# GDN heads of a hybrid GLA / gated DeltaNet block: output with values on the partitions, norm sums on 32x32 blocks

## The chip, the cores and the metric

The kernel runs on one core of one Trainium2 chip. The metric is the device time of one execution in microseconds, as the median of the runs shown. The core has five engines with a queue of instructions each: TensorE (PE; its weight loads are listed as PEld), VectorE (DVE), ScalarE (ACT), GpSimd (POOL) and SyncE (SP). DMAs are issued from the queues of SP, ACT and POOL. All data is float32; large products are made in three passes from a high and a low part of each operand (float32r), small ones directly in float32, which the trace shows as two passes ("x2").

## The reference, cut to what matters

The block takes 1024 tokens of 1024 channels through a GLA branch, a gated DeltaNet (GDN) branch, a gated merge and an MLP. The change concerns the end of the GDN branch: 8 heads with 128 keys and 128 values each. Per head, in chunks (the kernel uses chunks of 128 tokens, eight of them):

```python
v_new = uu - einsum('bhcd,bhdv->bhcv', ww, state)
o = einsum('bhcd,bhdv->bhcv', qd, state) + einsum('bhij,bhjv->bhiv', at, v_new)
state = dc[..., None, None] * state + einsum('bhcd,bhcv->bhdv', ks, v_new)
...
o_d = rms_norm(o_d, gdn_onorm_w) * jax.nn.silu(d_g.reshape(bsz, s, GDN_HEADS, GDN_DV))
y_d = o_d.reshape(bsz, s, GDN_V) @ w_branch_gdn
```

`rms_norm` divides each token of a head by the root of the mean square over its 128 values. The queries are L2-normalised in the reference; the kernel leaves the query unnormalised and brings its sum of squares in at the norm of the output instead: the sum of squares of the output over 128, plus the query's sum of squares (with its own epsilon) times 128 epsilon, is what the root is taken of.

## The kernel before, in words

All products are interleaved by a clock. `dense_b` (L475) makes one 128x1024 projection tile: for each of eight k it issues six matmuls of 512 columns and then calls `tick()` (L382), which adds one to the clock and issues everything that is due. `at(dt, fn)` (L371) puts a function on the agenda for `dt` steps ahead; what is due at the same step is issued in the order in which it was registered. In `gdn_head` (L906) `on(t, fn)` means step `t` counted from the head's own beginning.

One head takes 24 steps, three projections of eight steps: query, value, gate (`psq`, `psv`, `psg`). What the head does with them reaches into the steps of the next head: its state chain runs from step 24 to 47, and its finish behind that. So step 53 of one head is step 29 of the next one's chain. A head's instructions:

- steps 0 to 17: loads of the solved key matrices, of the decay and of two rows spread over all partitions (`eg`, `ke`, L1012 to L1016), the convolution of the query (`conv_silu`, three VectorE operations on 1024 columns), scores `attT` (L979).
- steps 15 to 33: the query's sums of squares. ScalarE squares into `qj`, VectorE transposes 32x32 blocks and sums (`token_part`, L992, steps 28 and 30), a product with `quad`, a matrix of 32x32 identities, adds up the four blocks of 32 partitions (`token_total`, L1000), and four VectorE operations bring that to one column per chunk, `vq`.
- steps 24 to 47, the chain: `c0(t)`, `c1(t)`, `c2(t)` (L1033 to L1070) at steps 24+3t, 25+3t, 26+3t for chunk t. `c0` transposes the values on TensorE and adds `ke` times the state, ScalarE scales that to `rs`; `c1` multiplies by the solved matrix `U`, ScalarE makes `vn` twice (scaled, and plain); `c2` makes the state's product (`kt`), VectorE writes the new state `st` from it (for t = 0 ScalarE copies it), and then the output `po` of the chunk, with `attT` and the decayed query `qd` as weights and `vn` and the old state as the moving operand: tokens on the partitions, values along the row. The state that VectorE writes at step 26+3t is needed by `c0` at step 27+3t.
- steps 35 and 47: `results` (L1075): ScalarE squares each 128x128 block of the output with a sum (`so`), and copies `po` to `ob`.
- step 26 to 28: the gate `sg` (ScalarE's tanh, then two VectorE operations).
- step 48 `norm` (L1083), eleven VectorE operations on 128x8; step 50 `scale`, one of 128x1024; steps 52 and 53 `fin` (L1092), four transposes on TensorE each; VectorE multiplies their result by the norm's weight and the gate into `sg` in two operations (steps 53, 54); step 56 the store to `od_d`.

Head 6 finishes later: `late` moves its second `results` by 7 steps, `end` its norm by 27, `f_` its `fin` by 32; head 7's `fin` is moved by 6. After head 7 the branch products begin (`branch`, L1698; `gla_plan`, L1596): step 24 of head 7 is their step 0, each of the seven products has eight steps of six matmuls, and their operands are split by ScalarE (`x_cast`, `w_cast`) and VectorE (`x_low`, `w_low`).

From the first GDN head on TensorE, VectorE and ScalarE keep the written order (L1454); SP and GpSimd do from head 7 on (L1797), before that a planner at compile time places their DMAs where its own estimate has them ready. Tiles come from shared pools: 30 tiles of 128x1024 in the pool `w4`, 16 of which hold the normalised input until the last projection, two `U`; four PSUM banks in `pa`, four more as two pairs in `pm`.

Of the kernel before, what the change touches and what calls it, by code (L numbers as in the profile page):

```python
# [20 lines left out]
EPS = 1e-6  # L21
# [29 lines left out]
def block_kernel(ctx: ExitStack, tc: tile.TileContext, x, c, ada_w, ada_b, pre_mix_w, post_mix_w,  # L51
# [36 lines left out]
            DMA.dma_start(dbg[name] if dst is None else dst(dbg[name]), src)  # L88


    def rsqrt(v, n):

        if n == 64:
            r, t = t4((128, n), p="rs"), t4((128, n), p="rt")
        else:
            r, t = small(n, "rs"), small(n, "rt")
        V.tensor_scalar(t.bitcast(I32), v.bitcast(I32), 1, None, ALU.logical_shift_right)
        V.tensor_scalar(r.bitcast(I32), t.bitcast(I32), -1.0, float(0x5F3759DF), ALU.mult, ALU.add)

        V.tensor_mul(t, r, r)  # L100
        V.tensor_mul(t, t, v)
        V.scalar_tensor_tensor(t, t, -10.0 / 3, t, ALU.add, ALU.mult)
        V.scalar_tensor_tensor(r, t, 5.0, r, ALU.add, ALU.mult)
        V.tensor_mul(t, r, r)
        V.scalar_tensor_tensor(t, t, -27.0 / 1024, v, ALU.mult, ALU.mult)
        last["rs"] = V.scalar_tensor_tensor(r, t, 9.0 / 16, r, ALU.add, ALU.mult).ins
        return r
# [794 lines left out]

    oa_d = [dr.tile([2, 128, 1024], F32, name=f"oa_d{i}") for i in range(4)]
    od_d = [dr.tile([2, 128, 1024], F32, name=f"od_d{i}") for i in range(4)]

    def gdn_head(h, then=None):  # L906

# [65 lines left out]
        psq = dense_b(h_rhs)  # L973

        q = conv_silu(psq, h, 8)
        vq = small(8, "vq")
        z = {}

        def att(hf):  # L979
# [17 lines left out]
            V.transpose(z["t"][:, h_], z["qj"][:, h_])  # L997
            V.reduce_sum(z["r"][:, hf * 16:(hf + 1) * 16], r3(z["t"][:, h_], 16), axis=mybir.AxisListType.X)

        def token_total():  # L1000
            ps = pat()
            T.matmul(ps[:, 0:32], quad.rearrange("p a b -> p (a b)"), z["r"], start=True, stop=True)

            def columns():
                for i in range(4):
                    V.tensor_scalar(vq[32 * i:32 * i + 32],
                                    ps[32 * i:32 * i + 32, 0:32].rearrange("p (t c) -> p c t", c=4)[:, i], EPS, None, ALU.add)

            on(33, columns)

        ktok, eg = t4(p="kt", tag="hd"), t4(p="eg")
        DMA.dma_start(ktok, kt_d[h])  # L1012
        DMA.dma_start(eg, gc_d[h].partition_broadcast(128))
# [9 lines left out]
        on(15, lambda: V.tensor_tensor(qd, q, eg, ALU.mult))  # L1023
        on(28, lambda: token_part(0))
        on(30, lambda: token_part(1))
        on(32, token_total)
        psv = dense_b(h_rhs)

        vv = conv_silu(psv, 16 + h, 16, 1)
        so = small(8, "so")  # L1030
        c = {"st": None}

        def c0(t):  # L1033
# [18 lines left out]
        def c2(t):  # L1052
            sl = slice(t * 128, (t + 1) * 128)
            i, hf, st, vs, vn = t % 4, t // 4, c["st"], c["vn"][:, 0:128], c["vn"][:, 128:256]
            if t < NT - 1:
                pS = c["pv"][:, 256:384]
                T.matmul(pS, ktok[:, sl], vs, start=True, stop=True)
                sn = c["st"] = sm.tile([128, 128], F32, tag="st", name=nm("st"), bufs=3)
                if t:
                    V.scalar_tensor_tensor(sn, st, decB[:, h * 8 + t:h * 8 + t + 1], pS, ALU.mult, ALU.add)  # L1060
                else:
                    A.copy(sn, pS)
            if i == 0:
                c["po"] = pat()
            po = c["po"]
            T.matmul(po[:, i * 128:(i + 1) * 128], z["att"][:, sl], vn, start=True, stop=(t == 0))
            if t:
                T.matmul(po[:, i * 128:(i + 1) * 128], qd[:, sl], st, start=False, stop=True)
            if i == 3:
                on(47 + late if hf else 35, lambda: results(hf, po))  # L1070

# [3 lines left out]
        def results(hf, po):  # L1075
            if not hf:
                c["ob"] = t4(p="ob")
            for t in range(hf * 4, hf * 4 + 4):
                A.activation(c["ob"][:, t * 128:(t + 1) * 128], po[:, t % 4 * 128:(t % 4 + 1) * 128], AF.Square,
                             accum_out=so[:, t:t + 1])  # L1080
            A.copy(c["ob"][:, hf * 512:(hf + 1) * 512], po)

        def norm():  # L1083

            V.tensor_scalar(so, so, 1.0 / 128, None, ALU.mult)
            V.scalar_tensor_tensor(so, vq, 128.0 * EPS, so, ALU.mult, ALU.add)
            c["rf"] = rsqrt(so, 8)

        def scale():
            V.tensor_tensor(r3(c["ob"]), r3(c["ob"]), colb(c["rf"], 8), ALU.mult)  # L1090

        def fin(hf):  # L1092
            pt, h_ = pat(), slice(hf * 512, (hf + 1) * 512)
            for i in range(4):
                t = hf * 4 + i
                T.transpose(pt[:, i * 128:(i + 1) * 128], c["ob"][:, t * 128:(t + 1) * 128], ident)
            on(53 + f_ + hf, lambda: V.scalar_tensor_tensor(sg[:, h_], pt, don, sg[:, h_], ALU.mult, ALU.mult))
            if hf:
                on(56 + f_, lambda: (DMA if h == 7 else A).dma_start(od_d[h // 2][h % 2], sg))
                dump("odT", sg, lambda t: t[h * 128:(h + 1) * 128, :])  # L1100

        for t in range(NT):
            on(24 + 3 * t, lambda t=t: c0(t))
# [1 line left out]
            on(26 + 3 * t, lambda t=t: c2(t))  # L1105
        if then:
            then()
        on(48 + end, norm)
        on(50 + end, scale)
        on(52 + f_, lambda: fin(0))  # L1110
        on(53 + f_, lambda: fin(1))
        psg = dense_b(h_rhs)

        sg = t4(p="si")
# [1359 lines left out]
```

## Time and profile before

| | us |
|---|---|
| median of 3 runs (lowest, highest) | 1893.22 (1891.84, 1896.31) |
| profiled execution, device time | 1890.98 |
| its span, first to last instruction | 1889.3 |
| TensorE busy | 1864.9 (99%) |
| VectorE busy | 1376.1 (73%) |
| ScalarE busy | 893.7 (47%) |
| GpSimd busy | 149.7 (8%) |

The GDN heads lie between about 570 and 978 us, the branch products behind them. TensorE's granted clock is 0.999 over the span. In rows of the order in time the columns are: start, time from the first start to the last end of the row, engine, source line (always the line of the helper that issues), operation, output and inputs by the program's names, sizes, and how many instructions the row holds; in brackets, how long the engine had been idle and what ended that. `pa` and `pm` are the PSUM tiles. `kt` is the `c2` product for the state, `ident,ob` the transposes of `fin`, `sqr,quad` the product of `token_total`, `si` the tile of the gate, `cv` that of a convolution.

### The profile page before, as it was taken

How to read it: one execution, taken by the hardware profiler on the slowest of the kernel's cores; microseconds unless marked ns; L12 is line 12 of the kernel's file. 1: busy time of each engine (PE TensorE's matmuls, PEld its weight loads, DVE VectorE, ACT ScalarE, POOL GpSimd, SP SyncE). 2: the span in 40 equal slices, each digit the busy share in tenths (PEclk: the TensorE clock that was granted, in tenths of full speed). 3: DMA queues.
4: the chain of work that ended last, by engine and by line, in shares of the span. 5: the costliest groups of instructions: out<-in, count | busy, mean ns of one | idle time of the engine just before them, and what ended most of it. 6: DMA issues, size and time to landing. Idle time of an engine off the chain costs nothing. (4 is left out here: it accounts for less than half of the span.)

```text
span 1889.3 us, 26430 instructions
## 1 busy us (share of the span) xinstructions
PE 1864.9 (99%) x10169; PEld 1563.8 (83%) x10169; DVE 1376.1 (73%) x2127; ACT 893.7 (47%) x1619; POOL 149.7 (8%) x138
## 2 busy tenths in 40 slices
PE   7999999999999999999999999999999999999998
PEld 5788888989898888888888888878888888888886
DVE  5664834868766666766788778976788877777887
ACT  5574324252333444444664555578644446433333
POOL 2120110110110000000101001000021220000001
PEclk9999999999999999999999999999999999999999
DMA  9685673223124444443869666246667668252425
GB/s 310 219 258 184 160 145 102 68 80 122 56 80 150 129 132 137 133 134 123 257 169 240 200 157 197 80 155 225 221 203 237 231 213 318 71 223 105 163 101 100
DMA packets 252318, 311.17 MB, mean 165 GB/s; under 512 B 72514, under 2 KB 178192, under 8 KB 252192
## 3 DMA queue, kind: packets, MB, share of 16 engines
q1 hardware_dynamic: 222464, 274.67, 45.2%
q0 software_dynamic: 13456, 19.80, 6.0%
q10 hardware_dynamic: 16272, 15.02, 2.4%
q8 instruction: 80, 1.31, 0.3%
q14 instruction: 46, 0.38, 0.1%
HBM read 229.05 MB, written 80.39 MB: 164 GB/s over the span
## 5 line engine op out<-in xcount | busy, mean ns | idle before, releaser
L38 PE MATMUL pm<-hH,wH 128*128 128x512 f32 x864 | 286.7, 413 | 0.0
L38 PE MATMUL pm<-hL,wH 128*128 128x512 f32 x864 | 268.6, 392 | 0.0
L38 PE MATMUL pm<-hH,wL 128*128 128x512 f32 x864 | 267.4, 391 | 0.0
L38 PE MATMUL pm<-oH,wB 128*128 128x512 f32 x672 | 214.7, 394 | 0.0
L38 PE MATMUL pa<-w,yH 128*128 128x512 f32 (+1 forms) x696 | 212.3, 387 | 0.0
L38 PEld LDWEIGHTS pm<-hL,wH 128*128 128x128 f32 x864 | 162.2, 188 | 36.5
L38 PEld LDWEIGHTS pm<-hH,wL 128*128 128x128 f32 x864 | 162.1, 188 | 36.4
L38 PEld LDWEIGHTS pm<-hH,wH 128*128 128x128 f32 x864 | 145.1, 190 | 17.0 <-issue 0.2
L38 DVE TENSOR_TENSOR w<-raw,w 128x512 fp32r<-128x512 f32 (+1 forms) x144 | 125.6, 875 | 41.5 <-ACT w L38 40.5
L38 PEld LDWEIGHTS pa<-w,yH 128*128 128x128 f32 x696 | 130.2, 188 | 26.7 <-DVE ya L38 0.4
L38 PEld LDWEIGHTS pm<-oH,wB 128*128 128x128 f32 x672 | 126.2, 188 | 26.0 <-DMA wB<-in_w_branch_gla_dram 0.5
L38 ACT CAST w<-raw 128x512 fp32r<-128x512 f32 (+1 forms) x144 | 99.6, 712 | 89.3 <-DVE raw L38 80.2
L38 PE MATMUL pa<-w,yL 128*128 128x512 f32 (+1 forms) x348 | 134.6, 387 | 0.0
L38 PE MATMUL pm<-oL,wB 128*128 128x512 f32 x336 | 131.0, 390 | 0.0
L38 PE MATMUL pa<-oB,w 128*128 128x512 f32 x480 | 112.1, 391 | 2.4 <-ACT oB L38 1.1
L38 ACT CAST wH<-raw 128x1024 fp32r<-128x1024 f32 x62 | 64.5, 1048 | 97.3 <-PE pm L38 48.7
L38 PEld LDWEIGHTS pa<-oB,w 128*128 128x128 f32 x480 | 89.7, 188 | 22.2 <-DVE oB L38 1.8
L38 DVE SCALAR_TENSOR_TENSOR cv<-pm,ccol,cv 128x1023 f32<-128x1023 f32 (+2 forms) x72 | 92.1, 1279 | 13.7 <-ACT cv L38 12.3
L38 DVE TENSOR_TENSOR wL<-raw,wH 128x1024 fp32r<-128x1024 f32 x62 | 75.4, 1220 | 34.6 <-ACT wH L38 34.5
L38 PE MATMUL pm<-oT,w 128*128 128x512 f32 x384 | 90.8, 389 | 0.0
L38 PE MATMUL pa<-oT,w 128*128 128x512 f32 x384 | 90.8, 389 | 0.0
L38 DVE TENSOR_TENSOR ya<-pa,ya 128x512 f32<-128x512 f32 (+1 forms) x83 | 55.9, 682 | 43.7 <-PE pa L38 43.7
(402 smaller groups left out, 3739.4 us busy)
## 6 DMA issues: line engine op xcount, KB each, us to landing
yL<-y_d SPq DMA_DIRECT2D x53, 512.0 KB, 7.1
raw<-in_mlp_w_dram SPq DMA_DIRECT2D x23, 1024.0 KB, 6.1
raw<-in_w_in_dram SPq DMA_DIRECT2D x18, 1024.0 KB, 7.3
raw<-in_w_in_dram SPq DMA_DIRECT2D x32, 512.0 KB, 4.9
araw<-in_ada_w_dram SPq DMA_DIRECT2D x32, 512.0 KB, 3.9
raw<-in_mlp_w_dram SPq DMA_DIRECT2D x18, 512.0 KB, 5.8
araw<-in_ada_w_dram SPq DMA_DIRECT2D x32, 256.0 KB, 6.4
sl<-sg_d SPq DMA_DIRECT2D x16, 512.0 KB, 7.1
```

Of the source, the lines that this page charges most:

```text
L38: r = fn(*args, **kw)
```

## The change

In `c2` weights and moving operand change places: the output is made with values on the partitions and tokens along the row. The transposes of `fin` and the product with `quad` with its four column reads are gone. `results` copies only, and squares the whole head at once when its second half is there (`sqo`). The squares are transposed and summed in blocks of 32x32 by VectorE, as the query's are (`turn`, `sums`, steps 49 to 52). `norm` (step 53) adds the query's sums, brings the four blocks of partitions together with three copies and three additions on 32x32, takes the root there in the nine operations of `rsqrt`, transposes the block and stores it to a row of 1024 in DRAM (`on_d`, one for each head). `rows` (step 57) loads that row into all 128 partitions; `scale` (step 55) multiplies output, weight and gate into `sg`, and `fin` (step 62) multiplies `sg` by the row; the store follows at step 63. The shifts `late`, `end` and `f_` of heads 6 and 7 stay as they are.

```diff
--- before.py
+++ after.py
@@ -88,9 +88,11 @@
             DMA.dma_start(dbg[name] if dst is None else dst(dbg[name]), src)
 
 
-    def rsqrt(v, n):
-
-        if n == 64:
+    def rsqrt(v, n, rt=None):
+
+        if rt:
+            r, t = rt
+        elif n == 64:
             r, t = t4((128, n), p="rs"), t4((128, n), p="rt")
         else:
             r, t = small(n, "rs"), small(n, "rt")
@@ -902,6 +904,7 @@
 
     oa_d = [dr.tile([2, 128, 1024], F32, name=f"oa_d{i}") for i in range(4)]
     od_d = [dr.tile([2, 128, 1024], F32, name=f"od_d{i}") for i in range(4)]
+    on_d = [dr.tile([1024], F32, name=f"on_d{h}") for h in range(8)]
 
     def gdn_head(h, then=None):
 
@@ -973,7 +976,6 @@
         psq = dense_b(h_rhs)
 
         q = conv_silu(psq, h, 8)
-        vq = small(8, "vq")
         z = {}
 
         def att(hf):
@@ -996,17 +998,6 @@
             h_ = slice(hf * 512, (hf + 1) * 512)
             V.transpose(z["t"][:, h_], z["qj"][:, h_])
             V.reduce_sum(z["r"][:, hf * 16:(hf + 1) * 16], r3(z["t"][:, h_], 16), axis=mybir.AxisListType.X)
-
-        def token_total():
-            ps = pat()
-            T.matmul(ps[:, 0:32], quad.rearrange("p a b -> p (a b)"), z["r"], start=True, stop=True)
-
-            def columns():
-                for i in range(4):
-                    V.tensor_scalar(vq[32 * i:32 * i + 32],
-                                    ps[32 * i:32 * i + 32, 0:32].rearrange("p (t c) -> p c t", c=4)[:, i], EPS, None, ALU.add)
-
-            on(33, columns)
 
         ktok, eg = t4(p="kt", tag="hd"), t4(p="eg")
         DMA.dma_start(ktok, kt_d[h])
@@ -1023,11 +1014,10 @@
         on(15, lambda: V.tensor_tensor(qd, q, eg, ALU.mult))
         on(28, lambda: token_part(0))
         on(30, lambda: token_part(1))
-        on(32, token_total)
         psv = dense_b(h_rhs)
 
         vv = conv_silu(psv, 16 + h, 16, 1)
-        so = small(8, "so")
+        so = small(32, "so", 2)
         c = {"st": None}
 
         def c0(t):
@@ -1063,9 +1053,9 @@
             if i == 0:
                 c["po"] = pat()
             po = c["po"]
-            T.matmul(po[:, i * 128:(i + 1) * 128], z["att"][:, sl], vn, start=True, stop=(t == 0))
+            T.matmul(po[:, i * 128:(i + 1) * 128], vn, z["att"][:, sl], start=True, stop=(t == 0))
             if t:
-                T.matmul(po[:, i * 128:(i + 1) * 128], qd[:, sl], st, start=False, stop=True)
+                T.matmul(po[:, i * 128:(i + 1) * 128], st, qd[:, sl], start=False, stop=True)
             if i == 3:
                 on(47 + late if hf else 35, lambda: results(hf, po))
 
@@ -1075,29 +1065,46 @@
         def results(hf, po):
             if not hf:
                 c["ob"] = t4(p="ob")
-            for t in range(hf * 4, hf * 4 + 4):
-                A.activation(c["ob"][:, t * 128:(t + 1) * 128], po[:, t % 4 * 128:(t % 4 + 1) * 128], AF.Square,
-                             accum_out=so[:, t:t + 1])
             A.copy(c["ob"][:, hf * 512:(hf + 1) * 512], po)
+            if hf:
+                c["sq"] = t4(p="sqo")
+                A.activation(c["sq"], c["ob"], AF.Square)
+
+        def turn(hf):
+            if not hf:
+                c["t"] = t4(p="sqt")
+            h_ = slice(hf * 512, (hf + 1) * 512)
+            V.transpose(c["t"][:, h_], c["sq"][:, h_])
+
+        def sums(hf):
+            h_ = slice(hf * 512, (hf + 1) * 512)
+            V.reduce_sum(so[:, hf * 16:(hf + 1) * 16], r3(c["t"][:, h_], 16), axis=mybir.AxisListType.X)
 
         def norm():
 
-            V.tensor_scalar(so, so, 1.0 / 128, None, ALU.mult)
-            V.scalar_tensor_tensor(so, vq, 128.0 * EPS, so, ALU.mult, ALU.add)
-            c["rf"] = rsqrt(so, 8)
+            b = t4(p="sog")
+            V.tensor_scalar(z["r"], z["r"], 128.0 * EPS, 32.0 * EPS * EPS, ALU.mult, ALU.add)
+            V.scalar_tensor_tensor(so, so, 1.0 / 128, z["r"], ALU.mult, ALU.add)
+            g = [b[0:32, i * 32:(i + 1) * 32] for i in range(6)]
+            for i in range(3):
+                V.tensor_copy(g[i], so[32 * i + 32:32 * i + 64, :])
+            V.tensor_add(g[0], g[0], so[0:32, :])
+            V.tensor_add(g[1], g[1], g[2])
+            V.tensor_add(g[0], g[0], g[1])
+            V.transpose(g[5], rsqrt(g[0], 32, g[3:5]))
+            DMA.dma_start(on_d[h].rearrange("(b i) -> b i", i=32), g[5])
+
+        def rows():
+            c["row"] = t4(p="row")
+            DMA.dma_start(c["row"], on_d[h].partition_broadcast(128))
 
         def scale():
-            V.tensor_tensor(r3(c["ob"]), r3(c["ob"]), colb(c["rf"], 8), ALU.mult)
-
-        def fin(hf):
-            pt, h_ = pat(), slice(hf * 512, (hf + 1) * 512)
-            for i in range(4):
-                t = hf * 4 + i
-                T.transpose(pt[:, i * 128:(i + 1) * 128], c["ob"][:, t * 128:(t + 1) * 128], ident)
-            on(53 + f_ + hf, lambda: V.scalar_tensor_tensor(sg[:, h_], pt, don, sg[:, h_], ALU.mult, ALU.mult))
-            if hf:
-                on(56 + f_, lambda: (DMA if h == 7 else A).dma_start(od_d[h // 2][h % 2], sg))
-                dump("odT", sg, lambda t: t[h * 128:(h + 1) * 128, :])
+            V.scalar_tensor_tensor(sg, c["ob"], don, sg, ALU.mult, ALU.mult)
+
+        def fin():
+            V.tensor_mul(sg, sg, c["row"])
+            on(f_ + 63, lambda: (DMA if h == 7 else A).dma_start(od_d[h // 2][h % 2], sg))
+            dump("odT", sg, lambda t: t[h * 128:(h + 1) * 128, :])
 
         for t in range(NT):
             on(24 + 3 * t, lambda t=t: c0(t))
@@ -1105,10 +1112,12 @@
             on(26 + 3 * t, lambda t=t: c2(t))
         if then:
             then()
-        on(48 + end, norm)
-        on(50 + end, scale)
-        on(52 + f_, lambda: fin(0))
-        on(53 + f_, lambda: fin(1))
+        for t, fn in enumerate((lambda: turn(0), lambda: sums(0), lambda: turn(1), lambda: sums(1))):
+            on(49 + late + t, fn)
+        on(53 + end, norm)
+        on(55 + end, scale)
+        on(57 + end, rows)
+        on(62 + f_, fin)
         psg = dense_b(h_rhs)
 
         sg = t4(p="si")
```

## The prediction, made before the result was known

> **What bounds the kernel now.** I read the page first, for the busy times, then the waits of TensorE in the delta-rule heads, then a table of stretches, then the order in time of each engine. Times are microseconds.
>
> ```profile
> span 1889.3 us, 26430 instructions
> PE 1864.9 (99%) x10169; PEld 1563.8 (83%) x10169; DVE 1376.1 (73%) x2127; ACT 893.7 (47%) x1619; POOL 149.7 (8%) x138
> ```
>
> ```profile
> PE pa L38 <- DVE st L38: 0.6, 1, 0.6
> 675.00:730.00 55.00, 55.00 (x344) 46.73 (x343) 38.83 (x60) 26.19 (x64) 0.00 (x0) 1.00 0.44 133
> 950.00:1010.00 60.00, 59.95 (x297) 49.36 (x296) 53.90 (x76) 32.44 (x58) 3.67 (x3) 1.00 0.71 199
> ```
>
> The first fence is the page: TensorE (PE) is busy 99% of the span. In the second, the first row says what TensorE waited for between 565 and 1010, the heads and the start of the branch products: one wait of 0.6 in 445, for VectorE (DVE) to write the state `st`. The two others give the busy time by engine in a stretch of heads (TensorE 55.00 of 55.00, VectorE 38.83) and in the stretch with the last head and the first products (TensorE 59.95 of 60, VectorE 53.90). So work taken from TensorE is time won one for one, as long as nothing makes it wait; VectorE has room on the average in the heads and hardly any behind them.
>
> What can make it wait is the state chain. VectorE runs in written order here, and each `st` is needed by TensorE's product `st,ke` one step later. Order in time of one regular head (chain of head 3, finish of head 2), TensorE:
>
> ```profile
> 702.08 0.39 PE L38 MATMUL pa<-vn,kt 128*128 128x128 f32 x2
> 705.63 0.60 PE L38 MATMUL pa<-ident,ob 128*128 128x128 f32 x4
> 706.06 0.39 PE L38 MATMUL pa<-rs,U 128*128 128x128 f32 x2
> 707.68 0.60 PE L38 MATMUL pa<-ident,ob 128*128 128x128 f32 x4
> 708.12 0.39 PE L38 MATMUL pa<-vn,kt 128*128 128x128 f32 x2
> 710.31 0.39 PE L38 MATMUL pa<-st,ke 128*128 128x128 f32 x2
> 713.54 0.30 PE L38 MATMUL pa<-sqr,quad 128*128 128x32 f32 x2
> 713.68 0.47 PE L38 MATMUL pa<-vn,kt 128*128 128x128 f32 x2
> ```
>
> The `kt` rows are the chain's steps 26 and 29, the `ident,ob` rows the eight transposes of the finished head, `st,ke` at 710.31 the first use of the state that VectorE writes after 708.12. The same chain in head 0, where no earlier head is being finished, so without those transposes; TensorE, then VectorE:
>
> ```profile
> 608.98 0.39 PE L38 MATMUL pa<-vn,kt 128*128 128x128 f32 x2
> 616.32 0.39 PE L38 MATMUL pa<-st,ke 128*128 128x128 f32 x2
> ```
>
> ```profile
> 612.37 0.70 DVE L38 STREAM_TRANSPOSE sqt<-qj 128x512 f32<-128x512 f32 x1
> 613.11 0.69 DVE L38 TENSOR_REDUCE sqr<-sqt 128x16 f32<-128x512 f32 x1
> 613.72 0.68 DVE L38 SCALAR_TENSOR_TENSOR si<-si,pm 128x512 f32<-128x512 f32 x1
> 614.58 0.35 DVE L38 SCALAR_TENSOR_TENSOR st<-st,decB,pa 128x128 f32<-128x128 f32 x1 [0.19 <-PE pa L38]
> ```
>
> From `kt` to `st,ke` it takes 710.31 - 702.08 = 8.23 in a regular head and 616.32 - 608.98 = 7.34 here. VectorE is done with the gate at 613.72 + 0.68 = 614.40, that is 5.42 after `kt`, and `st` starts 0.18 later, as soon as its product is there. That is the whole cushion of a chain without the transposes: 0.18, and about 1.4 from the end of `st` (614.93) to 616.32.
>
> **The change part by part.**
>
> TensorE loses the eight transposes of each head: 706.06 - 705.63 = 0.43 and 708.12 - 707.68 = 0.44, together 0.87. It loses the product with `quad`, two passes whose start moves the next by 713.68 - 713.54 = 0.14 and whose row lasts 0.30; I take 0.22 (bounds 0.14 and 0.30). 1.09 a head, times 8: **-8.7** (bounds -8.1 and -9.4). It holds if TensorE stays the engine that sets the pace.
>
> The exchange of operands in step c2 costs nothing I can see: as many passes of 128 columns. What was moving (`vn`, `st`) becomes the weights and must be there earlier, and it is:
>
> ```profile
> 701.15 0.26 ACT L38 COPY vn<-pa 128x128 f32<-128x128 f32 x1
> ```
>
> ScalarE's copy of `vn` ends at 701.41, and the products of that step begin at 702.08. Bounds 0 and, if a weight load could no longer run ahead, eight times the copy's 0.26 a head, 17; I take 0, since 0.67 lies between.
>
> ScalarE loses eight squares with sum and gains one square over 1024 columns; it waits for TensorE in the heads, so 0.
>
> VectorE is where the price is. Per head the change takes away the four column reads, the broadcast scaling's place (another 128x1024 operation of the same kind stands in for it) and two read-backs, and adds two transposes and two sums of the squares (steps 49 to 52), a longer `norm` (step 53 in place of 48), and a 128x1024 product with the row (step 62). Step 53 of a head is the step of the next head's second state, and what the earlier head registered comes first: `norm` now stands in front of that `st`. Today it stands five steps earlier, where no state is written by VectorE. What it costs today (first and last of its eleven operations), and then small operations of 64 columns, dependent (first two rows) and independent (last two):
>
> ```profile
> 698.96 0.17 DVE L38 TENSOR_SCALAR so<-so 128x8 f32<-128x8 f32 x1 [2.00 <-ACT ob L38]
> ...
> 700.99 0.17 DVE L38 SCALAR_TENSOR_TENSOR rs<-rt,rs 128x8 f32<-128x8 f32 x1
> ```
>
> ```profile
> 179.29 0.22 DVE L38 TENSOR_TENSOR rt<-rs 128x64 f32<-128x64 f32 x1
> 179.55 0.22 DVE L38 TENSOR_TENSOR rt<-rt,ssK 128x64 f32<-128x64 f32 x1
> 182.23 0.22 DVE L38 TENSOR_TENSOR rbC<-rs,betaC 128x64 f32<-128x64 f32 x1
> 182.36 0.22 DVE L38 SCALAR_TENSOR_TENSOR beC<-beC,rs 128x64 f32<-128x64 f32 x1
> ```
>
> Ten steps from 698.96 to 700.99 are one operation of 8 columns every 0.20, and 2.2 with the last one's 0.17. The new `norm` has 18 on 32 columns: two on the sums, three copies and three additions to bring the four blocks together, nine for the root, one transpose. Dependent operations of 64 columns follow at 0.26, independent ones at 0.13. Bounds: 18 x 0.13 = 2.3 and 18 x 0.26 = 4.7. Nearly all depend on the one before; 32 columns lie nearer to 8 than to 64, so some 0.22, less for the copies: I take 3.7.
>
> [...]
>
> Now the chain of heads 1 to 6, counted from `kt` of step 26 at the pace of head 0. VectorE is through with the gate at 5.42, with one more sum in front of it (613.72 - 613.11 = 0.61) at 6.03 (the other sum and the two transposes come before the gate, where the old `norm` and scaling were), with `norm` at 9.73, with `st` (0.35) at 10.08. How soon TensorE goes on then, and that this very wait does stop it, is shown by the one wait of before:
>
> ```profile
> 945.02 0.34 DVE L38 SCALAR_TENSOR_TENSOR st<-st,decB,pa 128x128 f32<-128x128 f32 x1
> 945.41 0.49 PE L38 MATMUL pa<-st,ke 128*128 128x128 f32 x2 [0.58 <-DVE st L38]
> ```
>
> 945.41 - 945.36 = 0.05. So `st,ke` can start at 10.13 in place of 7.34: a stall of 2.8, in six heads: **+16.8** (bounds with `norm` at 2.3 and 4.7: 1.4 and 3.8 a head, +8.4 and +22.8). Head 0 has no finish beside it, and head 6 is finished behind the last chain. The modulation sum (`aacc`), which ran behind the old `norm`, goes earlier and costs nothing. Later in the head the idle time of VectorE before `st` takes up the row product.
>
> The row: `norm` ends 9.7 after `kt`. Nearest rows for the store and the load:
>
> ```profile
> a<-a_d SPq DMA_DIRECT2D x7, 128.0 KB, 2.5
> eg<-gc_d SPq DMA_DIRECT2D x8, 512.0 KB, 4.7
> 723.48 0.34 SPq L38 DMA_DIRECT2D araw<-in_ada_w_dram  x1
> ```
>
> 2.5 + 4.7 and the issues make some 7.5. Six steps took 713.68 - 702.08 = 11.6, 1.93 each, so step 62, twelve steps after that `kt`, comes 12 x 1.93 + 2.8 - 0.9 = 25 behind it and 15 behind `norm`. I cost the wait at 0; if it isn't covered, see the third rival. The new tiles share 30 buffers, 16 of them held by the normalised input; one more tile lives through steps 57 to 62 and the gate 7 steps longer. If one were missing, ScalarE's next write would wait for a tile that TensorE frees a step later; I bound that by one `st` late as above (0.6, the wait at 945.41) in six heads, 0 and 4, and take 0, since a late load or write has steps to spare.
>
> Last head and branch products. Step by step the work of head 6 now falls into head 7's chain, the two norms among the first products:
>
> ```profile
> 949.38 0.35 DVE L38 SCALAR_TENSOR_TENSOR st<-st,decB,pa 128x128 f32<-128x128 f32 x1 [0.42 <-PE pa L38]
> 952.27 0.68 DVE L38 TENSOR_SCALAR vq<-pa 32x8 f32<-32x8 f32 x4
> 955.60 0.35 DVE L38 SCALAR_TENSOR_TENSOR st<-st,decB,pa 128x128 f32<-128x128 f32 x1
> 956.54 0.39 PE L38 MATMUL pa<-st,ke 128*128 128x128 f32 x2
> 978.35 0.17 DVE L38 TENSOR_SCALAR so<-so 128x8 f32<-128x8 f32 x1 [4.17 <-ACT ob L38]
> 993.92 0.74 DVE L38 SCALAR_TENSOR_TENSOR si<-pa,vcol,si 128x512 f32<-128x512 f32 x1
> 996.38 1.21 DVE L38 SCALAR_TENSOR_TENSOR z<-sl,pm 128x1024 f32<-128x1024 f32 x1
> 1001.84 0.61 PE L38 MATMUL pm<-oH,wB 128*128 128x512 f32 x2
> ```
>
> Head 6's transposes and sums, 2 x (0.74 + 0.61) = 2.7, come in front of `st` at 949.38 and 955.60. Idle time there (0.42 in front of 949.38) and the column reads (0.68) take up 1.1. 1.6 late, against 956.54 - 955.95 = 0.6 less the 0.2 by which TensorE is earlier: **+1.2** (0 to 2). Then `z` at 996.38 reads the banks that the product behind it overwrites from 1002.07 (second of the pair at 1001.84): 4.5 to spare, 2.7 once the 16 transposes before it (1.8) are gone. In front of `z` VectorE has 2.7 more for head 7, 2 x (3.7 - 2.2) = 3.0 more for the norms and two read-backs less (0.74 each): 4.2 late, a stall of 1.5, and I add 0.5 for the second half of the product, whose `z` comes a little later still: **+2**. Bounds 0, if VectorE fills the 4.2 in which it now waits before 978.35, and 7, since SP is in written order there and the norms' stores stand in front of the gates that `z` needs.
>
> Sum: -8.7 + 16.8 + 1.2 + 2 = **+11.3**. The profiled execution took 1890.98 (its span 1889.3, 1.7 around it), 2.2 below the median 1893.22. 1890.98 + 11.3 = 1902.3 for such an execution, 1904.5 against the median, which I predict.
>
> **The rivals.**
>
> *TensorE's saving is the whole story* (faster). It needs `norm` to fit the cushion: 6.03 + norm + 0.40 below 7.34, a `norm` of 0.9, or `st` being put ahead of it. For it: VectorE idles 16 of 55 in a stretch. Against: eleven smaller operations take 2.2, and what an earlier head registered stands first throughout the trace (`norm` precedes the modulation sum of its step). 1893.2 - 8.7 = 1884.5.
>
> *The small operations overlap* (no change). At the independent spacing, `norm` 2.3: 6 x 1.4 - 8.7 = -0.3, and some 1 in the products: 1894. For it: 0.13 between 182.23 and 182.36. Against: the chain of the root at 0.20. [...]
>
> *The row comes late.* If the load goes out behind the one that SP holds until 723.48, it lands at 723.48 + 1.9 (the shift by then) + 0.3 + 4.7 = 730.4, where step 62 is due at 702.08 + 25 = 727.1; the product with the row then stops VectorE in front of that step's `st`, which has 1.4 to spare: 1.9 in six heads, 11 more, 1916. For it: SP issues in one order, and that row waits for VectorE. Against: store and load fit twice into the 15.
>
> **How the numbers follow.** Forecast 0.69, row late 0.10, overlap 0.08, saving alone 0.13. A measurement of this kernel can tell 0.2%, 3.8, from no change. Faster 0.13, same 0.08, slower 0.79. The forecast's own range, from the bounds of the terms, is 1897 to 1914; to leave out no more than 2 in 10 the range reaches from 1889, between overlap and saving, to 1920, above the late row.
>
> **What would show it.** Right: TensorE waits for `st` once in each of heads 1 to 6, 2.8 each; the period of a head grows from 24 x 1.93 = 46 by 2.8 - 1.1 = 1.7; `norm` one operation each 0.2; no idle time of VectorE before that `st`; a wait for `z` among the first products. Wrong: `st` of step 53 ahead of `norm` or `norm` below 1.5; heads shorter by 1.1; waits at `st` of step 62 (the row) or of ScalarE for buffers.

## The result, and the profile after the change

The changed kernel took 1920.45 us (median of four runs, 1919.81 to 1922.3) against 1893.03 for the kernel before: a ratio of 1.0144, 95% interval 1.0126 to 1.0161. It is slower by 27.4 us where 11.3 were forecast: the direction was right, the size was not. All times below are in microseconds.

The page of the changed kernel, its profiled execution (1922.3, of which the span is 1920.6):

```profile
PE 1868.6 (97%) x10089; PEld 1561.3 (81%) x10089; DVE 1398.5 (73%) x2175; ACT 884.1 (46%) x1499; POOL 152.1 (8%) x138
```

TensorE has 80 recorded products fewer, and yet 3.7 more of busy time (1864.9 before), in a span 31.3 longer (1889.3 before, 1920.6 after). So it did not only wait more: some of its products also took longer. What it waited for from 565 to 1010 (first row) and from 1010 to 1100 (total, times, longest):

```profile
PE pa L38 <- DVE st L38: 14.7, 7, 2.4
PE pm L38 <- DMA wB<-in_w_in_dram: 9.9, 1, 9.9
PE pm L38 <- DVE z L38: 1.3, 2, 0.8
PE pm L38 <- DVE U L38: 1.3, 1, 1.3
```

Before, there was one wait for `st` of 0.6 and none of the other three. The forecast place is the first row: six waits of 2.35 to 2.38, and in the last head the one of 0.58 as before. VectorE in order of time, in the head that the prediction showed (its chain is head 2's, counted from 0, and head 1 is being finished; the prediction called them 3 and 2):

```profile
711.72 0.17 DVE L38 TENSOR_SCALAR sqr<-sqr 128x32 f32<-128x32 f32 x1
...
715.17 0.20 DVE L38 STREAM_TRANSPOSE sog<-sog 32x32 f32<-32x32 f32 x1
715.31 0.29 DVE L38 SCALAR_TENSOR_TENSOR st<-st,decB,pa 128x128 f32<-128x128 f32 x1
```

The eighteen operations of `norm` run from 711.72 to 715.31 without a gap, with `st` behind them: the forecast order, and 3.59 where 3.7 was forecast. TensorE at the same place:

```profile
713.03 0.27 PE L38 MATMUL pa<-ident,cv 128*128 128x128 f32 x1
715.66 0.49 PE L38 MATMUL pa<-st,ke 128*128 128x128 f32 x2 [2.35 <-DVE st L38]
...
720.56 0.38 PE L38 MATMUL pa<-vn,kt 128*128 128x128 f32 x2
```

It waits 2.35. Then comes what the forecast did not have: from `st,ke` to `vn,kt` it takes 720.56 - 715.66 = 4.90, where the same two rows of before, with the `quad` product between them, are 713.68 - 710.31 = 3.37 apart. A table of stretches behind two of the six waits shows why (columns: stretch, its length, busy time of PE, PEld, DVE, ACT and POOL, granted clock, DMA share, GB/s):

```profile
715.60:716.50 0.90, 0.84 (x5) 0.76 (x6) 0.87 (x3) 0.26 (x1) 0.00 (x0) 0.97 0.04 5
716.50:717.50 1.00, 1.00 (x4) 0.81 (x3) 1.00 (x2) 0.11 (x1) 0.00 (x0) 0.50 0.21 78
...
719.50:720.50 1.00, 1.00 (x5) 0.81 (x4) 0.33 (x1) 0.00 (x0) 0.00 (x0) 0.82 0.99 385
...
766.00:767.00 1.00, 0.97 (x5) 0.87 (x6) 0.97 (x2) 0.37 (x1) 0.00 (x0) 1.00 0.04 4
```

Behind the wait that ends at 715.66 the granted clock falls to 0.50 for 3.41, TensorE busy all the time; behind the next one, which ends at 766.03 and is as long (2.35), it stays at 1.00. The last section comes back to that. The second state of a chain on VectorE, in heads 0, 2, 3, 4 and 7:

```profile
615.11 0.35 DVE L38 SCALAR_TENSOR_TENSOR st<-st,decB,pa 128x128 f32<-128x128 f32 x1 [0.17 <-PE pa L38]
...
715.31 0.29 DVE L38 SCALAR_TENSOR_TENSOR st<-st,decB,pa 128x128 f32<-128x128 f32 x1
765.68 0.29 DVE L38 SCALAR_TENSOR_TENSOR st<-st,decB,pa 128x128 f32<-128x128 f32 x1
814.75 0.29 DVE L38 SCALAR_TENSOR_TENSOR st<-st,decB,pa 128x128 f32<-128x128 f32 x1
...
962.52 0.34 DVE L38 SCALAR_TENSOR_TENSOR st<-st,decB,pa 128x128 f32<-128x128 f32 x1
```

A head takes 50.37 from 715.31 to 765.68, where the clock fell, and 49.07 from 765.68 to 814.75, where it did not. The second of these two heads is 0.21 longer than the first in the kernel before too (755.54 to 802.75, 47.21, against 708.54 to 755.54, 47.00), so the low clock costs some 1.5 a head. From 615.11 to 962.52 it is 347.41; the same two rows of before (614.58 and 945.02, both in the prediction) are 330.44 apart. So the heads lose 17.0. Behind 962.52 there are 958.1 to the end, 944.3 before: 13.8 more are lost there, and that is the second thing that the forecast did not have. TensorE, SyncE's queue (SP) and ScalarE of the changed kernel, and then SP before:

```profile
1053.46 1.22 PE L38 MATMUL pm<-oH,wB 128*128 128x512 f32 x2 [9.90 <-DMA wB<-in_w_in_dram]
```

```profile
1007.57 0.33 SPq L38 DMA_DIRECT2D on_d<-sog  x1
...
1012.31 0.32 SPq L38 DMA_DIRECT2D on_d<-sog  x1
...
1016.56 5.69 SPq L38 DMA_DIRECT2D wq<-in_w_in_dram  x4
```

```profile
1025.74 1.05 ACT L38 CAST wB<-wq 128x1024 fp32r<-128x1024 f32 x1 [4.58 <-DMA wq<-in_w_in_dram]
...
1034.42 1.05 ACT L38 CAST wB<-wq 128x1024 fp32r<-128x1024 f32 x1 [6.53 <-DVE si L38]
```

```profile
989.49 5.34 SPq L38 DMA_DIRECT2D wq<-in_w_in_dram  x4
```

SP issues in written order. The loads of the `md` branch's weights (`wq`) now stand behind the two stores of `norm`'s result, heads 6 and 7, which wait for VectorE; they go out at 1016.56 instead of 989.49, 27 later, where the heads account for 17. ScalarE's cast waits 4.58 for them, the next one 6.53 behind the store of `od_d` in its own queue, and the first product of the `md` branch 9.9 for the weights (`wB`, which GpSimd's load completes when ScalarE has written it).

### The profile page after: what moved, and what is told of

Same layout as the page of the kernel before. It is cut to its first block, busy times and chain, and to the rows that moved or that the text cites. A ratio compares the mean times of both kernels' runs of the same rounds, so it can differ in the third digit from the quotient of the medians.

```text
span 1920.6 us, 26251 instructions
## 1 busy us (share of the span) xinstructions
PE 1868.6 (97%) x10089; PEld 1561.3 (81%) x10089; DVE 1398.5 (73%) x2175; ACT 884.1 (46%) x1499; POOL 152.1 (8%) x138
## 5 line engine op out<-in xcount | busy, mean ns | idle before, releaser
L38 PEld LDWEIGHTS pm<-hH,wH 128*128 128x128 f32 x864 | 146.2, 191 | 17.1 <-issue 0.2
```

The costliest lines, as they stand in the source:

```text
L38: r = fn(*args, **kw)
```

## The experiments

The theory after the result: (A) `norm`'s place ahead of `st` makes six waits; four of them also halve the clock; and (B) SP's order makes the 9.9. The rivals: the low clock comes from the exchanged products themselves; the wait moves on to another state when `norm` moves; the weights are late for ScalarE's sake. Differences below are against the kernel before in the same comparison.

**`norm` behind `st`.** At its step, `norm` is put on the list once more, so that it comes after all that is due there:

```
-        on(53 + end, norm)
+        on(53 + end, lambda: at(0, norm))
```

> The changed kernel with norm's 18 small operations put behind, not ahead of, what else is due at step 53, the next head's second st among it; nothing else moved. Theory A (the small operations ahead of st make the waits, and each wait of 2.35 us also halves TensorE's granted clock for some 3.5 us, which costs 1.7 us more): the six waits for st go, the clock stays at 1.00 behind the second c2, the head's period falls from 50.43 to about 46.3, and the time by 6 x 4.05 = 24 us to about 1896. Theory B (the waits for st are one thing, the low clock another, from the exchanged products): the waits go, the half clock stays, the time falls by 6 x 2.35 = 14 us to about 1906. Theory C (the work only moves the wait to the next st, three steps on): waits of about 2 us before the third c2, the time 1915 to 1920.

1910.66, ratio 1.0092 (1.0076 to 1.0108): +17.2 instead of +27.4. TensorE's waits, then VectorE around the chain of head 1, then the stretch behind the wait:

```profile
PE pa L38 <- DVE st L38: 10.0, 7, 1.6
PE pm L38 <- DMA wB<-in_w_in_dram: 9.1, 1, 9.1
```

```profile
660.65 0.34 DVE L38 SCALAR_TENSOR_TENSOR st<-st,decB,pa 128x128 f32<-128x128 f32 x1
...
668.79 0.35 DVE L38 SCALAR_TENSOR_TENSOR st<-st,decB,pa 128x128 f32<-128x128 f32 x1
```

```profile
669.20:670.20 1.00, 1.00 (x5) 0.89 (x6) 1.00 (x1) 0.42 (x2) 0.00 (x0) 1.00 0.95 356
```

Theory C held half: `st` at 660.65 is in time now, but VectorE still has `norm`, the sums, `scale` and the transposes of `U` to do before the third state, three steps on, which is late instead: six waits of 1.6. Behind all six the clock is 1.00. The price of one head's surplus work was moved and made smaller, not removed.

**The row's transfers on another queue.** In heads 6 and 7, GpSimd issues the store in `norm` and the load in `rows`:

```
-            DMA.dma_start(on_d[h]...
+            (G if h > 5 else DMA).dma_start(on_d[h]...
-            DMA.dma_start(c["row"], ...
+            (G if h > 5 else DMA).dma_start(c["row"], ...
```

> The changed kernel with the store and the load of the row issued by GpSimd instead of SP in heads 6 and 7; nothing else moved. Theory A (SP, which issues in written order, held the loads of md's weights behind the row's store that waits for norm): the 9.9 us that md's first product waits for wB goes, and with it the half clock behind it (about 1.7 us): about 1909. Theory B (the weights are late because ScalarE's queue is held by the later store of od_d, or GpSimd's by what is before it): the wait stays within 2 us of 9.9, the time within 2 us of 1920.

1910.86, ratio 1.0095 (1.0079 to 1.0111): +17.4. Waits, and SP:

```profile
PE pm L38 <- DMA wB<-in_w_in_dram: 2.2, 1, 2.2
```

```profile
1007.27 7.08 SPq L38 DMA_DIRECT2D wq<-in_w_in_dram  x4
```

The loads go out 9.3 earlier and the wait falls from 9.9 to 2.2, with the waits for `st` as they were (14.7 in all): theory A, SP's order. What is left, 2.2, is a wait for GpSimd's load of `wB`; what holds that load is not shown by this run.

**Both.** The two edits above in one kernel:

> Both edits at once: norm behind what else is due at its step, and the row's store and load of heads 6 and 7 issued by GpSimd. If the two losses are separate they add: 1920.4 - 24 - 11.6 = 1885, below the kernel before (1893) by about the 8.7 us that TensorE saves. If the wait for wB only takes the place of time that the heads' waits gave, or the GpSimd queue is as late as SP's, it stays at the 1896 of the first edit alone or above.

1901.14, ratio 1.0043 (1.0027 to 1.0059): +7.6. The first edit had given back 10.2, the second 10.0, both give 19.8: the two losses are separate and add up. It is not the 1885 that was expected, because the first edit only moved the waits: six of 1.6 are left in the heads, and the kernel is still slower than before.

**TensorE's part alone**, on the kernel before:

```
-            T.matmul(po[...], z["att"][:, sl], vn, ...
+            T.matmul(po[...], vn, z["att"][:, sl], ...
-                T.matmul(po[...], qd[:, sl], st, ...
+                T.matmul(po[...], st, qd[:, sl], ...
-            pt, h_ = pat(), slice(hf * 512, (hf + 1) * 512)
-            for i in range(4): ... T.transpose(pt[...], c["ob"][...], ident)
+            h_ = slice(hf * 512, (hf + 1) * 512)
+            pt = c["ob"][:, h_]
```

> The kernel before with TensorE's part of the change alone: the operands of c2's two output products exchanged, and fin's eight transposes a head left out (fin then reads ob itself; norm, its sums and its scale stay as they were, so the values are normed along the wrong axis: the computation is not the reference's). Theory A (TensorE sets the heads' pace, and the exchange is free): 8 x 0.87 = 7.0 us less, about 1886, and the head's period 46.99 - 0.87 = 46.1. Rival (the exchange costs what the transposes gave, or the chain of products and evictions sets the pace): 1893 within 2 us.

1884.36, ratio 0.9954 (0.9936 to 0.9971): -9.2. Two second states and TensorE's waits from 565 to 1100:

```profile
707.30 0.35 DVE L38 SCALAR_TENSOR_TENSOR st<-st,decB,pa 128x128 f32<-128x128 f32 x1 [0.19 <-PE pa L38]
...
753.39 0.35 DVE L38 SCALAR_TENSOR_TENSOR st<-st,decB,pa 128x128 f32<-128x128 f32 x1 [0.19 <-PE pa L38]
```

```profile
PE pa L38 <- DVE st L38: 0.6, 1, 0.6
PE pa L38 <- ACT rs L38: 0.4, 1, 0.4
```

The head's period is 46.09, 0.91 below the 47.00 of before (708.54 to 755.54), with no new wait in the heads but the 0.4 of the last one: the exchange of operands is free, and what TensorE saves is won in full. It is the room that the rest of the change has to live in.

**Does a wait of this kind halve the clock, whoever makes it?** The kernel before, with dependent small operations on VectorE ahead of the second state of heads 1 to 6; 18 of them, then 24:

```
+        def idle():
+            d = small(8, "du")
+            for _ in range(18):
+                V.tensor_scalar(d, don.to_broadcast([128, 8]) if _ == 0 else d, 1.0, None, ALU.mult)
+        if h < 6:
+            on(53, idle)
```

> The kernel before, with a chain of 18 dependent VectorE operations of 128x8 added at step 53 of heads 0 to 5, ahead of the next head's second st; their result is not used. VectorE is idle 1.05 us there and TensorE needs st some 1.4 us after its end, so 18 x 0.2 = 3.6 us are to leave a wait of about 1.2 us in each of six heads. Theory A (the granted clock falls only behind a wait of about 2 us or more): the clock stays 1.00, the time rises by 6 x 1.2 to 1.6 = 7 to 10 us, to 1900 to 1903. Theory B (any wait of over a microsecond halves the clock): 6 x 2.9 = 17 us more, 1911.

> The same with 24 operations instead of 18: 24 x 0.2 = 4.8 us, a wait of about 2.4 us in each of six heads. Theory A (a wait of this length halves the granted clock for some 3.5 us behind it, whatever made it): PEclk near 0.50 behind the second c2, the time up by 6 x (2.4 + 1.7) = 25 us, to about 1918. Theory B (the low clock in the changed kernel came from its exchanged products, not from the wait): the clock stays 1.00 and the time rises by 6 x 2.4 to 2.8 = 14 to 17 us, to 1907 to 1910.

18: 1900.45, ratio 1.0038 (1.0024 to 1.0052), +7.1. 24: 1914.81, ratio 1.0112 (1.0097 to 1.0127), +21.4. Waits and one stretch of the first, then of the second:

```profile
PE pa L38 <- DVE st L38: 7.6, 8, 1.1
```

```profile
664.30:665.30 1.00, 1.00 (x7) 0.88 (x8) 1.00 (x2) 0.37 (x1) 0.00 (x0) 1.00 0.09 33
```

```profile
PE pa L38 <- DVE st L38: 14.5, 8, 2.3
```

```profile
667.00:668.00 1.00, 1.00 (x5) 0.91 (x4) 1.00 (x3) 0.00 (x0) 0.00 (x0) 0.50 0.00 0
668.00:669.00 1.00, 1.00 (x4) 0.80 (x3) 0.97 (x3) 0.52 (x2) 0.00 (x0) 0.50 0.08 33
```

Six more operations, 1.2 of VectorE's time in each of six heads, cost 14.3. With 18 the six waits are 1.05 each, the clock stays at 1.00, and the time rises by little more than the waits (6.3). With 24 they are 2.28 each (13.7), and the clock falls to 0.50 behind five of the six. A head takes 51.03 with the fall (664.88 to 715.91) and 49.43 without it (715.91 to 765.34), 1.6 less; five times 1.6 make 8.0, and with the 13.7 that is 21.7 for the 21.4 measured. Nothing of the change is in these kernels, so the low clock belongs to the wait, not to the exchanged products.

**Places with room.** In the kernel with both edits, heads 0 to 5 end later: `scale`, `norm`, `rows` and `fin` at steps 57, 64, 66 and 71, in VectorE's idle stretches.

```
-        on(53 + end, lambda: at(0, norm)) ...
+        n_, c_, r_, e_ = (53 + end, 55 + end, 57 + end, 62 + f_) if h > 5 else (64, 57, 66, 71)
+        on(n_, lambda: at(0, norm))
+        on(c_, scale)
+        on(r_, rows)
+        on(e_, fin)
```

> The kernel of both edits, with the end of heads 0 to 5 moved into VectorE's idle stretches: scale from step 55 to 57 (behind the chain's third c2), norm from 53 to 64 (where VectorE sat idle 3.4 us ahead of the sixth st), the row's load from 57 to 66, fin from 62 to 71. Theory A (VectorE's order is all that is left between this kernel and TensorE's saving): the six waits for st of 1.59 us go and nothing comes in their place; the period falls from 48.05 to about 46.2, the time from 1901.1 by 6 x 1.85 = 11 to about 1890. Theory B (the 32x32 work has no free place: wherever it stands a later st or a tanh that waits for one more live buffer pays for it): waits of 1 us or more appear elsewhere and the time stays above 1896.

1910.4, ratio 1.0085 (1.007 to 1.01): +17.0, worse than without it. TensorE's waits, and one of ScalarE's:

```profile
PE pa L38 <- ACT rs L38: 8.4, 5, 1.7
PE pa L38 <- DVE st L38: 7.1, 2, 4.8
```

```profile
ACT cv L38 <- DMA on_d<-sog: 25.6, 5, 5.1
```

Theory B, and in the heads it is the buffer, not VectorE's order: in five heads ScalarE waits 5.1 for the buffer of the 32x32 blocks, which is free only when their store has landed, and TensorE then 1.7 for ScalarE. The other 7.1 are two waits in the last head: ahead of the longer one VectorE sits idle 3.19 and 1.45 for loads of the other branch's weights, and at its end the clock falls. Why those loads are late in this kernel is not shown. So the steps from 53 to 58 were tried next: `norm` at 58, where VectorE had been idle 2.1 before the fourth state, `scale` at 55, `rows` at 60, `fin` at 64.

```
-                                                                            else (64, 57, 66, 71)
+                                                                            else (58, 55, 60, 64)
-        on(e_, fin)
+        on(e_, fin if h > 5 else lambda: at(0, fin))
```

> The kernel of both edits with other places for heads 0 to 5: scale stays at step 55, norm goes from 53 to 58 (behind the third st and two of q's convolution taps, where VectorE sat idle 2.1 us and TensorE can wait 1.45 us more for the next st), the row's load from 57 to 60, fin from 62 to 64, behind the products of the attention, where VectorE sat idle 3.4 us. Theory A (a place with room in front of the next st and for the buffers is all that is missing): no wait for st or rs of over 0.5 us in heads 0 to 5, period about 46.2, time about 1890. Theory B (the 32x32 block's own buffer is the cost, since w4 has none to spare): waits for rs of 1 us and more remain, time 1896 or above.

And the same with `norm`'s blocks and the row in `ob`'s own buffer (heads 0 to 5):

```
-            b = t4(p="sog")
+            b = t4(p="sog") if h > 5 else c["ob"]
-            c["row"] = t4(p="row")
+            c["row"] = t4(p="row") if h > 5 else c["ob"]
```

> The same places, and in heads 0 to 5 norm's blocks and the row use ob's own buffer, which scale has read by then, in place of two new buffers. If live w4 buffers still cost (tanh's wait for a buffer that TensorE holds, 1.9 us at most, and the products' waits for rs behind it), this is 1 to 6 us faster than the kernel without it; if not, the two are within 1 us.

1892.34, ratio 0.9995 (0.9986 to 1.0005), and 1893.3, ratio 1.0003 (0.9993 to 1.0012): no different from the kernel before, nor from each other. The first one's waits from 565 to 1100, and two second states:

```profile
PE pm L38 <- DMA wB<-in_w_in_dram: 2.2, 1, 2.2
PE pa L38 <- DVE st L38: 1.8, 2, 1.2
PE pm L38 <- DVE U L38: 1.3, 1, 1.3
PE pm L38 <- DVE z L38: 1.0, 2, 0.8
```

```profile
707.23 0.34 DVE L38 SCALAR_TENSOR_TENSOR st<-st,decB,pa 128x128 f32<-128x128 f32 x1
...
753.41 0.34 DVE L38 SCALAR_TENSOR_TENSOR st<-st,decB,pa 128x128 f32<-128x128 f32 x1
```

The period is 46.18, as TensorE's part alone gave it (46.09), and one wait of 1.2 is left in the heads, in head 3, where four operations of another part stand in VectorE's way. At these places the buffers cost nothing. What eats the gain is behind the heads: 4.5 of waits for weights, `U` and `z`.

Two more edits aimed at the 1.2 and the 2.2: in head 2 the roots go behind the fourth state, and ScalarE issues head 6's `od_d` three steps later.

```
-            V.transpose(g[5], rsqrt(g[0], 32, g[3:5]))
+            if h == 2:
+                on(59, lambda: at(0, lambda: root(g)))
+            else:
+                root(g)
...
-            on(e_ + 1, ...
+            on(e_ + (4 if h == 6 else 1), ...
```

> The kernel with the row in ob's buffer, with two more edits. In head 2 the roots (ten of norm's eighteen operations) go behind the fourth st, one step after the sums, because there four more VectorE operations (2.7 us) of another part stand ahead of that st and left its only wait of 1.2 us in the heads. And ScalarE issues head 6's store of od_d three steps later, because its queue stood 9 us behind that store until VectorE had written si, and md's weight casts behind it. If both are the causes: the wait for st falls below 0.5 us, that for wB to about 0, and the time by about 1.7 + 1.3 = 3 us, to 1889 to 1891, below the kernel before (1893.2). If the weights are late for another reason (GpSimd's accumulating loads behind U), the wait for wB stays at 1 us or more and the time falls by 1 to 2 us.

1891.42, ratio 0.9993 (0.9983 to 1.0002). Waits from 565 to 1100:

```profile
PE pm L38 <- DMA wB<-in_w_in_dram: 1.7, 1, 1.7
...
PE pa L38 <- DVE st L38: 0.6, 1, 0.6
```

The 1.2 is gone; the wait for the weights is not, so `od_d` in ScalarE's queue was not its cause. Last, heads 6 and 7 were given back their old end (transposes, sums of columns, and operands as before), heads 0 to 5 keep the new one:

```
+        old = h > 5
...
+            T.matmul(po_, *((r_, l_) if old else (l_, r_)), ...
...
+        if old:
+            on(48 + end, norm_old)
+            on(50 + end, scale_old)
+            on(52 + f_, lambda: fin_old(0))
+            on(53 + f_, lambda: fin_old(1))
+        else: ...
```

> Heads 0 to 5 as in the kernel before this one (output by exchanged operands, norm's sums behind the fourth tap place, the row in ob's buffer), heads 6 and 7 as in the kernel before the change, transposes and all. If what is left of the loss is the larger VectorE work of heads 6 and 7 (norm, row and two more passes each) colliding with the branch products, the waits for z, U and wB go, and six heads keep 46.99 - 46.2 = 0.8 us each: 4.8 us under the kernel before, about 1888.5. If the products of the branches wait because the heads end earlier than their weights can come, the waits for wB stay above 1 us and the time is 1890 or more.

1890.21, ratio 0.9982 (0.9973 to 0.9991): faster than both kernels, by 3.4 (1.7 to 5.1) against the one before. Waits from 565 to 1100, and VectorE in head 7's chain:

```profile
PE pa L38 <- DVE st L38: 2.9, 2, 2.3
PE pa L38 <- ACT rs L38: 0.8, 1, 0.8
```

```profile
948.15 1.23 DVE L38 TENSOR_TENSOR raw<-wq,raw 128x1024 f32<-128x1024 f32 x1 [3.47 <-DMA wq<-in_w_branch_gla_dram]
```

The waits for `wB`, `U` and `z` are gone, so they belonged to the larger work of heads 6 and 7 on VectorE and the queues. In their place is one of 2.3 with 0.8 behind it: the last head's second state is written 5.1 earlier (939.97 against 945.02), and GpSimd's load of the other branch's weights, for which VectorE sits idle 3.47, goes out only 0.65 earlier (939.13 against 939.78). These waits are longer than the 1.4 that separates 3.4 from the 4.8 expected.

## Why the prediction was wrong in size

*TensorE's saving, -8.7, and the exchange at 0: right.* The transposes and the exchange alone gave 9.2 (interval 5.5 to 12.1), 0.91 a head where 0.87 was reckoned. The 0.22 of the `quad` product is there and is lost again: with `norm` at step 58 and no such product, the two stretches from `kt` to `kt` beside its place take 5.39 and 6.19, where they took 5.53 and 6.29 with it, but the next two take 6.42 and 7.27 instead of 6.20 and 7.18. There ScalarE's tanh, whose input VectorE has finished at 720.80, waits 1.89 for TensorE until 722.96, and the `vn` behind it is ready only at 724.43, for a product that starts at 724.48. By the kernel's text it can only be a buffer that TensorE still holds; so the buffers were not quite free.

*`norm` at 3.7, ahead of `st`, with no idle time: right* (3.59). The dependent operations of this chain follow each other some 0.2 apart (711.72 and 711.92, the first two), two additions that don't need each other 0.11 (712.74 and 712.85).

*The stall, 2.8 in six heads, +16.8: right in mechanism, a little too large* (waits of 2.35 to 2.38, 14.1 in all; from `kt` at 705.79 to `st,ke` at 715.66 it takes 9.87 where 10.13 was forecast, 2.5 over the 7.34). The head was forecast 1.7 longer and became 3.4 longer where the clock fell (50.38 against 47.00) and 1.9 where it did not (49.07 against 47.21).

*The step that failed first* is the one that followed the stall: TensorE was taken to go on at its pace, so that a late state cost its lateness. It costs its lateness, 1.5 more where the clock falls (four of six, 6.1), and some 0.4 in each head besides: 49.07 without the fall, less 2.37 of wait and the 46.30 that the same head takes with TensorE's part alone (753.39 to 799.70). Of this 0.4, 0.26 is at the wait itself: before, `st,ke` starts 0.11 behind the product in front of it, which lasts 0.27, and the next product follows 0.14 behind it; here that overlap is gone, and the next follows 0.24 behind. Another 0.09 is there without a wait (46.18 against 46.09). Together 14.1 + 6.1 + 2.4, less the 5.5 that TensorE's part alone saves between the same two rows (615.12 to 940.10, 324.98), make 17.1 for the heads' loss of 17.0.

*The row at 0: right* in the heads, where no product waited for it. *The buffers at 0: nearly right at the tried places* (1892.34 and 1893.3 with and without two of them, and the tanh's wait in both), but with no margin: at step 64 one buffer cost five waits of 1.7. *Head 7's +1.2* did not come: the wait for `st` there is 0.58, as before.

*The step that failed second* is the branch products, +2 with bounds 0 and 7. Its wait for `z` came, 0.8 and 0.5 where 1.5 and 0.5 were forecast; one of 1.3 for `U`, which the forecast did not name, came beside it. Its upper bound saw that "SP is in written order there and the norms' stores stand in front", but followed that queue only to the gates that `z` needs. The next entry of the same queue, the four loads of `md`'s weights, was not followed: 9.9 of wait and, with the clock at 0.50 for about four microseconds behind it, some 2 more. Moving the two transfers gave back 10.0. In the profiled executions the whole difference is 31.3, 20.0 above the forecast: 7.8 of it in the heads (17.0, where 16.8 less seven savings of 1.09 made 9.2) and 11.7 behind them (13.8, where 1.2 + 2 less one saving made 2.1); the last 0.5 lies ahead of them. The forecast's own range, 1897 to 1914, was too narrow for its terms as well: with the exchange and the buffers at 0 their bounds add up to -1.0 and +23.7, that is 1892 to 1917.

The rivals: "saving alone" (1884.5) was the right time for TensorE's part without the rest, 1884.36. "Row late" had the wrong transfer: not the row but what stood behind its store in SP's queue was late; that it named a time near the measured one (1916) is luck.

What stays open: what holds the last 1.3 to 2.2 of the wait for `wB` with the new end in heads 6 and 7; it goes when those heads get their old end. In the kernel with the two tuning edits GpSimd issues that load at 1018.70, right behind ScalarE's write of the same tile, and the product starts at 1024.32; ScalarE in its turn had waited 3.11 for TensorE, and why is not shown.

## What to carry to other kernels

Price a stall of the bound engine by its length, by what the clock does behind it (here 0.50 for 3.41, some 1.5 more, in four heads of six), and by what runs late after it; and follow a newly waiting DMA down its whole queue, past the one transfer that you had in mind to everything queued behind it, up to the first product that needs one of them. Work that is moved off the bound engine must be placed step by step against the next deadlines of the engine that takes it: the same eighteen operations cost 2.4 and a slower clock at one step, 1.6 at the next place in line, and nothing five steps later in five heads of six. And where the surplus has no place, as in the last two heads, doing the old thing there is better than doing the new one everywhere.

## What the runs showed that was not expected

The clock's fall. A wait of TensorE of 2.35 was followed by half clock in four cases of six in the changed kernel, one of 2.28 in five of six with 24 added operations, one of 2.36 in three of six with the row on GpSimd's queue. In tables of stretches of 0.5, each low stretch in the heads is 3.41 long, and the ends of those of one execution lie whole multiples of that apart (668.66, 719.86, 818.85 and 870.05 in the changed kernel: 51.20, 98.99 and 51.20, which are 15, 29 and 15 times 3.413). So the execution seems cut into fixed stretches of 3.41, and how a wait falls on them decides: the low stretch is the one behind the stretch that holds most of the wait. The largest part of each of the 18 waits that lies in one such stretch, worked out from these ends:

| kernel | clock fell behind | clock stayed at 1.00 |
|---|---|---|
| changed | 2.38, 2.35, 2.37, 2.26 | 1.79, 1.47 |
| 24 added operations | 2.04, 2.19, 2.23, 2.27, 2.28 | 1.87 |
| row on GpSimd's queue | 2.35, 2.06, 2.38 | 1.81, 1.46, 1.69 |

All 18 are parted by one line between 1.87 and 2.04 of 3.41. Waits that can't fill that much of a stretch, the six of 1.6 and the six of 1.05, were never followed by a fall. The line was drawn after the fact and not tried on a kernel made for it, but four other waits of over 2, from which it was not drawn, fit it. The clock stayed at 1.00 behind one of 2.19 (row on GpSimd's queue, at 1043.60) and one of 2.26 (places with room, at 951.30), with 1.21 and 1.41 in one stretch; it fell behind one of 4.83 (places with room, at 967.16) and, for three stretches, 1047.55 to 1057.79, at the one of 9.90 in the changed kernel; both fill at least one whole stretch.
